# Hybrid encoder step on one core: all attention projections beside stick-breaking, the recurrence started in the forgetting attention, and smaller staging edits

## The chip, the cores and the metric

The kernel runs on one NeuronCore of a Trainium2 chip. The metric is the device time of one execution in microseconds (us), the median over several runs. Engines are named as the profile names them: PE is TensorE's matmuls and PEld its weight loads, DVE is VectorE, ACT is ScalarE, POOL is GpSimd, and SP is the sync engine, which here only issues DMAs.

## The reference

One layer of a streaming encoder is computed for 1024 prompt rows and 64 sample rows of width 1024; the two groups share all weights, and the sample group has 256 cached rows. Cut to what matters:

```
u = rms_norm(x)
proj = u @ w_in            # q, k, v of three attentions, the inputs of the delta net, four gates of width 1024
A forgetting attention (fox): softmax(q k' / 8 + c_q - c_k), causal, c = cumsum(log_sigmoid(f))
B differential attention (diff): softmax1 - lam * softmax2, block-causal in chunks of 64, then rms_norm
C stick-breaking attention (sb): exp(log_sigmoid(z) + reversed cumsum of log_sigmoid(-z)), strictly causal
D gated delta net (gdn): conv, silu, l2norm, then per chunk of 64 rows:
    solve (I + m) sol = [v beta, k beta exp(g)]          # a triangular solve
    v_new = u_i - kc_i S;  o = q_i S + a_i v_new;  S = S exp(g_last) + k_i' v_new      # a recurrence over chunks
merged = sum_b sigmoid(gate_b) * (o_b @ w_branch[b])
x += merged @ w_out;  x += (silu(h wg) * (h wu)) wd, h = rms_norm(x);  y = rms_norm(x)
```

The new k, v, log-forget rows, the last state S and the last conv rows are outputs as well.

## The kernel before

All 1088 rows of u lie in SBUF as two f16 halves (a high part and a rest), and weights are split in the same way when they are loaded: `load_unit` reads a block of 256 columns, ACT writes `wh`, and DVE writes the rest `wl`. So each product is made of three matmuls.

The program has these stages. First come the norm, the projection of the delta net (`gdn_project`) and its first pass (`gdn_pass1`). Then come the three attentions in the order sb, fox, diff. Each attention loops over two pairs of heads, over nine row blocks in the order QORD (the long ones first), and over the two heads of the pair. For one head, PE makes the scores (`psc`), ACT and DVE make the weights (`st`), a transposing DMA issued by SP turns them (`pt`), and PE multiplies them with v (`pv` for sb and fox, `po` for diff). Behind the attentions comes the merge, in which each branch is multiplied by its branch weights (`ptb`), by its gate, and added into `mg`; then the output product (`pout`), the FFN and the last norm.

Three kinds of work have no fixed stage. `project(b)` makes q, k and v of an attention in 26 pieces of 24 matmuls of 256 columns; `put_q`, `put_k` and `put_v` split each piece with ACT and DVE, and SP writes it to DRAM. `spill_gates` makes the gates of all four branches in 96 pieces of 24 matmuls of 360 or 364 columns (`pgs`, lines 183 to 185); ACT copies each to a tile `ths`, and POOL writes it to DRAM, from where the merge reads it as `thg`. These two kinds are generators in the list `dense`. The list `side` has `gdn_solve`, the 30 steps of the triangular solve on DVE (tile X), and `gdn_seq`, the recurrence over 17 chunks, which makes small matmuls (`py`, `pu`, `pk`, `pog`, `pds`) and short DVE and ACT operations in turn. At each head (diff) or row block (sb, fox), `fill(us)` takes so many microseconds' worth of pieces from `dense`, by hand-set prices of 2.6 for a projection piece and 3.7 for a gate piece, and one step from `side`:

```
    def fill(us):
        debt[0] += us
        debt[0] = min(debt[0], us + 4.0)
        while dense and debt[0] > 0:
            c = next(dense[0], None)
...
        if side and next(side[0], None) is None:
            side.pop(0)
```

What is still in `dense` behind the attentions is issued by `drain(dense)`. The order that results from the code is only a priority: a scheduler places the instructions of each engine at build time, and on the chip each engine then works strictly in that order.

PSUM has eight banks: two for projections and gates (`pd`), three for scores (`psc`), one for `pv` and `po` (`pso`), and two for the delta net (`pgd`). SBUF pools are stacks: a pool opened in the place of a closed one has to wait for the last use of the old tiles.

Of the kernel before, what the change touches and what calls it, by code (L numbers as in the profile page):

```python
# [11 lines left out]
F32 = mybir.dt.float32  # L12
# [5 lines left out]
P = 128  # L18
D = 1024
KD = D // P  # L20
# [22 lines left out]

QORD = (7, 6, 5, 4, 3, 2, 8, 1, 0)

FILL_SB, FILL_FOX, FILL_DIFF, FILL_GDN = 0.0143, 0.0085, 0.0155, 8


def rows(t):
# [4 lines left out]
def tile_hybrid_encoder(ctx, tc, i, o):  # L54
# [809 lines left out]
    def gdn_solve():  # L864


        NP = 17 * NH
        with tc.tile_pool(name="gp2", bufs=1, side="right", reuse_waits="tile") as g2p:
            X = g2p.tile([NP, 2, 32, 32], F32, name="X")
            tmp = g2p.tile([NP, 512], F32, name="tmpx")  # L870
            gps.dma_start(X.rearrange("p b j i -> p b (j i)"), nd[0:17, :, 0:2].rearrange("n h b j i -> (n h) b (j i)"))
            for _ in range(3):
                yield 0.0
            for j in range(1, 31):
                r = 31 - j
                behind = tc.issue_after(at_mark[0].ins) if j == 1 else ExitStack()
                behind.__enter__()
                tj = tmp[:, :2 * j * r].rearrange("p (b c i) -> p b c i", b=2, c=j)
                tt(tj, bc(X[:, :, 0:j, j:j + 1], [NP, 2, j, r]), bc(X[:, :, j:j + 1, j + 1:32], [NP, 2, j, r]), ALU.mult)
                tt(X[:, :, 0:j, j + 1:32], X[:, :, 0:j, j + 1:32], tj, ALU.add)  # L880
                behind.__exit__(None, None, None)
                if j % 3 == 0:
                    yield 0.0
            for q in range(2):
                vec.memset(X[:, q].rearrange("p j i -> p (j i)")[:, 0:1024:33], 1.0)
            gps.dma_start(xd, X.rearrange("p b j i -> p (b j i)"))
            for q in range(2):
                vec.tensor_copy(tmp.rearrange("p (i j) -> p i j", j=32),
                                X[:, 0, :, 16 * q:16 * q + 16].rearrange("p j i -> p i j"))
                gps.dma_start(xtd[:, 512 * q:512 * q + 512], tmp)  # L890
# [2 lines left out]
        acopy(Sh, S32, 16.0)  # L893
        stt(Sl, S32, 16.0, Sh, ALU.mult, ALU.subtract)

    def gdn_seq(g3):
        ttbd = []
        for q in range(2):
            a = g3.tile([P, 2, NH, P], F16, name=f"ttbd{q}")
# [94 lines left out]
        for k, t in enumerate(order):  # L994
            after = load(order[k + 1]) if k + 1 < len(order) else None
            _, n, nch, u0, kc, kd, aa, qe, zt = here
            z4g = zt.rearrange("p (h e) -> p h e", h=NH)
            S32 = S32s if t == 8 else S32p
            if t in (8, 0):
                Sh, Sl = fresh_state()  # L1000
                new_state(S32, Sh, Sl)
            po = pgd("pog")
            pks = po[:, 256:512]
            for c in range(nch):
                sl = slice(64 * c, 64 * c + 64)
                e4 = eg[:, c, t * NH:(t + 1) * NH]
                for h in range(NH):
                    pe.matmul(pks[sl, h * 64:h * 64 + 64], lhsT=kc[:, h, sl], rhs=Sh[:, h], start=True, stop=False)
                    pe.matmul(pks[sl, h * 64:h * 64 + 64], lhsT=kc[:, h, sl], rhs=Sl[:, h], start=False, stop=True)
                S1 = g3.tile([P, NH, 64], F32, tag="S1", name="S1", bufs=2)  # L1010
                tt(S1, S32, bc(e4[:, :, None], [P, NH, 64]), ALU.mult)
                vn = g3.tile([P, NH, 64], F32, tag="vn", name="vn", bufs=2)
                vh = vhs[c]
                stt(vn[sl].rearrange("p h e -> p (h e)"), pks[sl, 0:256], -(2.0 ** -5),
                    u0[sl].rearrange("p h e -> p (h e)"), ALU.mult, ALU.add)
                acopy(vh[sl, 0], vn[sl])
                tt(vh[sl, 1], vn[sl], vh[sl, 0], ALU.subtract)
                pds = pgd("pds")
                for h in range(NH):
                    for q, (a, b) in enumerate(((0, 0), (0, 1), (1, 0))):  # L1020
                        pe.matmul(pds[:, h * 64:h * 64 + 64], lhsT=kd[:, a, h], rhs=vh[:, b, h], start=(q == 0), stop=(q == 2))
                for h in range(NH):
                    dst = po[sl, h * 64:h * 64 + 64]
                    pe.matmul(dst, lhsT=qe[:, h, sl], rhs=Sh[:, h], start=True, stop=False)
                    pe.matmul(dst, lhsT=qe[:, h, sl], rhs=Sl[:, h], start=False, stop=False)
                    pe.matmul(dst, lhsT=aa[:, 0, h], rhs=vh[:, 0, h], start=False, stop=False)
                    pe.matmul(dst, lhsT=aa[:, 0, h], rhs=vh[:, 1, h], start=False, stop=False)
                    pe.matmul(dst, lhsT=aa[:, 1, h], rhs=vh[:, 0, h], start=False, stop=True)
                stt(S32.rearrange("p h e -> p (h e)"), pds[:, 0:256], 2.0 ** -9, S1.rearrange("p h e -> p (h e)"), ALU.mult, ALU.add)
                Sh, Sl = fresh_state()  # L1030
                if not (t == 8 or (t == 7 and c == 1)):
                    new_state(S32, Sh, Sl)
                if c == 0 and after is not None:
                    here = prepare(*after)
                yield 0.0
            if t == 8:
                gps.dma_start(o["s_gdn_state"][0, 0].rearrange("h d e -> d h e"), S32[0:64])
            if t == 7:
                gps.dma_start(o["p_gdn_state"][0, 0].rearrange("h d e -> d h e"), S32[0:64])
            sq = g3.tile([P, NH, 64], F32, tag="sqo", name="sqo", bufs=1)  # L1040
            pov = po[:n, 0:256].rearrange("p (h e) -> p h e", h=NH)
            act.activation(sq[:n], pov, AF.Square)
            ss = g3.tile([P, NH], F32, tag="sso", name="sso", bufs=2)
            vec.tensor_reduce(out=ss[:n], in_=sq[:n], op=ALU.add, axis=AX.X)
            ts(ss[:n], ss[:n], 2.0 ** -18 / 64, EPS, ALU.mult, ALU.add, eng=gps)
            tt(ss[:n], ss[:n], mhb[:n, 0:NH], ALU.pow, eng=gps)
            tt(z4g[:n], z4g[:n], bc(ss[:n, :, None], [n, NH, 64]), ALU.mult)
            tt(z4g[:n], z4g[:n], pov, ALU.mult)
            os_ = g3.tile([P, 2, BW], F16, tag="osg", name="osg", bufs=2)
            acopy(os_[:n, 0], zt[:n])  # L1050
            tt(os_[:n, 1], zt[:n], os_[:n, 0], ALU.subtract)
            gps.dma_start(od["gdn"][t * P:t * P + n], os_[:n].rearrange("p l c -> p (l c)"))
# [3 lines left out]
    def spill_gates(b, sp, d2):  # L1056
        j = bidx[b]
        wu = load_unit([(w_in, 0, OFF_GATE + j * D + d2 * BW, BW)], BW)
        for m in range(2):
            d = 2 * d2 + m  # L1060
            for off, n in PIECES:
                pg = pd("pgs")
                gemm_a(pg, wu, m * P, uh, ul, off, n, KD)
                th = sp.tile([P, 364], F32, tag="ths", name="ths", bufs=2)
                with tc.high_priority():
                    acopy(th[:, :n], pg[:, :n], 0.5 * IWS)
                gps.dma_start(gtd[b][d * P:(d + 1) * P, off:off + n], th[:, :n])
                yield 3.7


    with tc.tile_pool(name="gp1", bufs=1, side="right", reuse_waits="tile") as g1p:
# [6 lines left out]
        gdn_project(xg)  # L1078
        ahead.clear()
        proj = [project(b) for b in ("sb", "fox", "diff")]  # L1080
        dense += proj[0:2]
        for w in gdn_pass1(g1p, xg):
            fill(w * FILL_GDN)
    drain(dense, proj[0])
# [6 lines left out]
    fill(16.0)  # L1091
    with tc.issue_after(pre.ins):
        attend_sb()
    drain(dense, proj[1])
    drain(dense, dense[0])
    cb_ = ExitStack()
    cb = cb_.enter_context(tc.tile_pool(name="cb", bufs=1, side="right", reuse_waits="tile"))
    dense.insert(0, proj[2])
    side.append(gdn_solve())
    attend_fox()  # L1100
    drain(dense, proj[2])
    drain(side)
    cb_.close()
    pj_.close()
    gd_, br_ = ExitStack(), ExitStack()
    g3 = gd_.enter_context(tc.tile_pool(name="gp3", bufs=1, side="right", reuse_waits="tile"))
    brps, branch = [], {}

    def load_branch(b):
# [8 lines left out]
        wbh = brp.tile([P, 2, D], F16, tag="wbh", name="wbh", bufs=2)  # L1118
        wbl = brp.tile([P, 2, D], F16, tag="wbl", name="wbl", bufs=2)
        for k in range(2):  # L1120
            w32 = wp.tile([P, 4, BW], F32, tag="w32", name="wb32", bufs=3)
            wv = w32.rearrange("p a b -> p (a b)")[:, :D]
            sync.dma_start(wv, i["w_branch"][0][j, k * P:(k + 1) * P])
            acopy(wbh[:, k], wv, WS)
            stt(wbl[:, k], wv, WS, wbh[:, k], ALU.mult, ALU.subtract)
# [2 lines left out]
    def open_merge():  # L1128
# [1 line left out]
        brps.append(br_.enter_context(tc.tile_pool(name="br", bufs=1, side="right", reuse_waits="tile")))  # L1130
        load_branch("sb")
        yield 0.0
        load_branch("fox")
        yield 0.0

    side += [gdn_seq(g3), open_merge()]
    attend_diff()
    drain(side)
    brp = brps[0]
# [17 lines left out]

    pbk = (psc, pgd, psc, pgd, psc)
    nb_ = [0]
    mg = [(brp if d < 3 else gt_pool).tile([P, T], F32, tag=f"mg{d}", name=f"mg{d}") for d in range(KD)]  # L1160
    order = ("sb", "fox", "diff", "gdn")
    for bi, b in enumerate(order):
        if b not in branch:
# [375 lines left out]
```

## Time and profile before

| | |
|---|---|
| time, median of 3 runs | 1920.94 us (1919.0 to 1921.34) |
| the profiled execution | 1923.47 us, of which the span from first to last instruction is 1921.5 us |
| mean granted TensorE clock | 0.954 of full speed |
| busy share of the span | PE 92%, PEld 65%, DVE 65%, ACT 45%, POOL 16% |

Busy shares are averages over stages with different limits, and a matmul's recorded time overlaps that of the next one. So the stages have to be read one by one: which engine is busy in each, at what clock, and what the others wait for.

### The profile page before, as it was taken

What the parts mean: (1) busy time and instruction counts of PE and PEld (TensorE: products, weight loads), DVE (VectorE), ACT (ScalarE), POOL (GpSimd) and SP (SyncE); (2) the same over time, 40 slices, a digit from 0 to 9 for tenths busy, and PEclk for the clock granted to TensorE, in tenths of its full rate; (3) what the DMA queues carried; (4) which work ended last, traced back from release to release, by engine and by line L of the source; (5) the groups of instructions that cost most, each with busy time, mean ns of one, the idle gap of its engine ahead of it and who ended that gap; (6) DMA issues with size and microseconds to landing.
All of it is one profiled execution on the core that took longest, in us unless ns stands there. A gap on an engine that the chain in (4) does not pass through costs nothing.

```text
span 1921.5 us, 36810 instructions
## 1 busy us (share of the span) xinstructions
PE 1767.0 (92%) x14364; PEld 1252.4 (65%) x14364; DVE 1249.0 (65%) x2589; ACT 868.2 (45%) x1819; POOL 310.3 (16%) x478
## 2 busy tenths in 40 slices
PE   7999898989977998766799889999999999999998
PEld 5678774656755565444466558886857758677573
DVE  7559773877776667889411997766646546556365
ACT  6335654998654455556522463433413314233142
POOL 2113341111001222212211661000000000000002
PEclk9999999999989999566899999999999999999999
DMA  6267789887989855444733955621211212112112
GB/s 222 44 108 218 224 234 215 168 179 155 208 191 210 183 148 128 94 108 84 262 107 103 280 153 144 121 83 34 78 44 45 67 32 79 45 45 67 33 45 99
DMA packets 412766, 244.28 MB, mean 127 GB/s; under 512 B 266278, under 2 KB 390450, under 8 KB 412456
## 3 DMA queue, kind: packets, MB, share of 16 engines
q1 hardware_dynamic: 398944, 205.67, 43.9%
q0 software_dynamic: 13648, 36.27, 6.5%
q8 instruction: 112, 1.84, 0.4%
q14 instruction: 62, 0.51, 0.1%
HBM read 123.39 MB, written 60.53 MB: 96 GB/s over the span
## 4 chain that ended last, share of the span: by engine, by line
PE 53%; DVE 8%; DMA 7%; issue 2%; ACT 1%; POOL 1%; SPq 0%; DVEq 0%; POOLq 0%; ACTq 0%
PE po L1461 12%; DMA pt<-st 4%; PE pgs L185 4%; PE pgs L183 3%; PE pgs L184 3%; PE pb L1345 3%; PE pb L1344 3%; PE pb L1346 3%; PE pc L1345 2%; PE pc L1346 2%; PE pa L1346 2%; PE pc L1344 2%; PE pa L1345 2%; PE pa L1344 2%; PE pout L165 1%
## 5 line engine op out<-in xcount | busy, mean ns | idle before, releaser
L183 PE MATMUL pgs<-u,wh 128*128 128x364 f16 (+1 forms) x768 | 245.1, 319 | 10.0 <-ACT ths L61 9.7
L184 PE MATMUL pgs<-u,wh 128*128 128x364 f16 (+1 forms) x768 | 245.2, 319 | 0.0
L185 PE MATMUL pgs<-u,wl 128*128 128x364 f16 (+1 forms) x768 | 244.7, 319 | 0.5 <-DVE wl L64 0.5
L1461 PE MATMUL po<-wh,hT 128*128 128x512 f16 (+1 forms) x792 | 238.1, 380 | 0.6 <-DVE x2a L64 0.6
L1461 PEld LDWEIGHTS <-hT 128*128 128x128 f16 (+1 forms) x1188 | 109.2, 99 | 120.0 <-issue 7.6
L64 DVE SCALAR_TENSOR_TENSOR x2a<-po,x2a 128x512 f32<-128x512 f32 x108 | 74.4, 689 | 141.6 <-PE po L1461 141.4
L61 ACT ACTIVATE wh<-w32f 128x1024 f16<-128x1024 f32 (+1 forms) x90 | 80.3, 926 | 160.6 <-PE po L1461 111.6
L1344 PE MATMUL pb<-X,wh 128*128 128x288 f16 (+1 forms) x528 | 147.1, 279 | 2.5 <-DMA X<-nsh 2.2
L1345 PE MATMUL pb<-X,wh 128*128 128x288 f16 (+1 forms) x528 | 147.2, 279 | 0.3 <-DMA X<-nsl 0.3
L1346 PE MATMUL pb<-X,wl 128*128 128x256 f16 (+1 forms) x528 | 146.3, 279 | 0.0
L64 DVE SCALAR_TENSOR_TENSOR wl<-w32f,wh 128x1024 f16<-128x1024 f32 (+1 forms) x90 | 94.6, 1065 | 79.2 <-ACT wh L61 79.1
L64 DVE SCALAR_TENSOR_TENSOR wl<-w,wh 128x1024 f16<-128x1024 f32 x62 | 74.8, 1229 | 108.8 <-ACT wh L61 80.3
L1461 PE MATMUL po<-wl,hT 128*128 128x512 f16 (+1 forms) x396 | 142.0, 379 | 0.0
L1344 PEld LDWEIGHTS <-wh 128*128 128x128 f16 x1232 | 120.5, 98 | 31.1 <-issue 2.3
L1345 PEld LDWEIGHTS <-wh 128*128 128x128 f16 x1232 | 120.5, 98 | 30.0 <-issue 2.4
L1346 PEld LDWEIGHTS <-wl 128*128 128x128 f16 x1232 | 120.5, 98 | 27.2 <-issue 0.9
L184 PEld LDWEIGHTS <-wh 128*128 128x128 f16 x912 | 89.6, 98 | 61.0 <-issue 11.8
L165 PE MATMUL pd<-wh,u 128*128 128x256 f16 (+1 forms) x448 | 123.8, 276 | 1.5 <-ACT e L61 1.5
L167 PE MATMUL pd<-wh,u 128*128 128x256 f16 (+1 forms) x448 | 123.5, 276 | 0.0
L166 PE MATMUL pd<-wl,u 128*128 128x256 f16 (+1 forms) x448 | 123.5, 276 | 0.0
L183 PEld LDWEIGHTS <-wh 128*128 128x128 f16 x912 | 89.7, 98 | 51.7 <-issue 1.7
L185 PEld LDWEIGHTS <-wl 128*128 128x128 f16 x912 | 89.6, 98 | 51.4 <-issue 1.2
(393 smaller groups left out, 4647.4 us busy)
## 6 DMA issues: line engine op xcount, KB each, us to landing
w<-in_w_in_dram SPq DMA_DIRECT2D x56, 512.0 KB, 5.3
w32f<-in_w_ffn_gate_dram SPq DMA_DIRECT2D x20, 512.0 KB, 4.9
w32f<-in_w_ffn_up_dram SPq DMA_DIRECT2D x20, 512.0 KB, 3.9
w32f<-in_w_ffn_down_dram SPq DMA_DIRECT2D x20, 512.0 KB, 4.1
xt<-in_x_prompt_dram SPq DMA_DIRECT2D x8, 512.0 KB, 6.8
wb<-in_w_branch_dram SPq DMA_DIRECT2D x8, 512.0 KB, 4.9
w<-in_w_out_dram SPq DMA_DIRECT2D x8, 512.0 KB, 4.9
x2a<-in_x_prompt_dram SPq DMA_DIRECT2D x8, 512.0 KB, 8.4
```

Source lines behind the costliest of these rows:

```text
L61: return act.activation(out, in_, AF.Copy, scale=scale)
L64: return vec.scalar_tensor_tensor(out=out, in0=in0, scalar=s, in1=in1, op0=op0, op1=op1)
L165: pe.matmul(ps[:n, :N], lhsT=a, rhs=wh[:, k, :N], start=(k == 0), stop=False)
L166: pe.matmul(ps[:n, :N], lhsT=a, rhs=wl[:, k, :N], start=False, stop=False)
L167: pe.matmul(ps[:n, :N], lhsT=b, rhs=wh[:, k, :N], start=False, stop=(k == K - 1))
L183: pe.matmul(ps[:, :n], lhsT=a, rhs=xh[:, k, off:off + n], start=(k == 0), stop=False)
L184: pe.matmul(ps[:, :n], lhsT=a, rhs=xl[:, k, off:off + n], start=False, stop=False)
L185: mm = pe.matmul(ps[:, :n], lhsT=b, rhs=xh[:, k, off:off + n], start=False, stop=(k == K - 1))
L1344: pe.matmul(ps[:, :n], lhsT=wh[:, k], rhs=xh_, start=(start and k == 0), stop=False, skip_group_check=not start)
L1345: pe.matmul(ps[:, :n], lhsT=wh[:, k], rhs=xl_, start=False, stop=False, skip_group_check=not start)
L1346: mm = pe.matmul(ps[:, :n], lhsT=wl[:, k], rhs=xh_, start=False, stop=(k == 3), skip_group_check=not start)
L1461: pe.matmul(ps[h * n:h * n + n], lhsT=hts[k + h][:, a, tk:tk + n], rhs=w[:, k + h], start=(k == 0 and a == 0 and w is wh), stop=(k + nh >= ...
```

## The change

- `dense` gets all three projections at the start; before, that of diff was put in front of the list when the fox attention began. All of them now end within the sb attention, and their pool `pj` is closed there.
- `gdn_solve`, `gdn_seq` and `open_merge` stand in `side` from the start of the fox attention on; before, `gdn_seq` was put there when the diff attention began. The solve has fewer yields (2 for 3, and one in 4 steps for one in 3). The fill of the fox attention falls from 0.0085 to 0.006 per column.
- `pds`, the product for the state's update, no longer takes a bank of its own, but lies in the second half of that of `pog`.
- `ths` has four buffers for two. The branch weights of sb are staged in the tiles of `mg0` and `mg1`, `mg2` moves to another pool, and the branch weights of fox are no longer loaded ahead of the merge's loop.

```diff
-FILL_SB, FILL_FOX, FILL_DIFF, FILL_GDN = 0.0143, 0.0085, 0.0155, 8
+FILL_SB, FILL_FOX, FILL_DIFF, FILL_GDN = 0.0143, 0.006, 0.0155, 8
...
-            for _ in range(3):
+            for _ in range(2):
                 yield 0.0
             for j in range(1, 31):
...
-                if j % 3 == 0:
+                if j % 4 == 0:
                     yield 0.0
...
-    def gdn_seq(g3):
+    def gdn_seq(stack):
+        g3 = stack.enter_context(tc.tile_pool(name="gp3", bufs=1, side="right", reuse_waits="tile"))
...
             po = pgd("pog")
-            pks = po[:, 256:512]
+            pks = pds = po[:, 256:512]
...
-                pds = pgd("pds")
...
-                th = sp.tile([P, 364], F32, tag="ths", name="ths", bufs=2)
+                th = sp.tile([P, 364], F32, tag="ths", name="ths", bufs=4)
...
         proj = [project(b) for b in ("sb", "fox", "diff")]
-        dense += proj[0:2]
+        dense += proj
...
         attend_sb()
-    drain(dense, proj[1])
     drain(dense, dense[0])
-    cb_ = ExitStack()
-    cb = cb_.enter_context(tc.tile_pool(name="cb", bufs=1, side="right", reuse_waits="tile"))
-    dense.insert(0, proj[2])
-    side.append(gdn_solve())
-    attend_fox()
-    drain(dense, proj[2])
-    drain(side)
-    cb_.close()
     pj_.close()
     gd_, br_ = ExitStack(), ExitStack()
-    g3 = gd_.enter_context(tc.tile_pool(name="gp3", bufs=1, side="right", reuse_waits="tile"))
+    cb = gd_.enter_context(tc.tile_pool(name="cb", bufs=1, side="right", reuse_waits="tile"))
...
-            w32 = wp.tile([P, 4, BW], F32, tag="w32", name="wb32", bufs=3)
-            wv = w32.rearrange("p a b -> p (a b)")[:, :D]
+            if b == "sb":
+                wv = brp.tile([P, T], F32, tag=f"mg{k}", name="wb32")[:, :D]
+            else:
+                w32 = wp.tile([P, 4, BW], F32, tag="w32", name="wb32", bufs=3)
+                wv = w32.rearrange("p a b -> p (a b)")[:, :D]
...
         load_branch("sb")
         yield 0.0
-        load_branch("fox")
-        yield 0.0
-
-    side += [gdn_seq(g3), open_merge()]
+
+    side += [gdn_solve(), gdn_seq(gd_), open_merge()]
+    attend_fox()
     attend_diff()
...
-    mg = [(brp if d < 3 else gt_pool).tile([P, T], F32, tag=f"mg{d}", name=f"mg{d}") for d in range(KD)]
+    mg = [(brp if d < 2 else gt_pool).tile([P, T], F32, tag=f"mg{d}", name=f"mg{d}") for d in range(KD)]
```

How the order on the engines moves is seen at three places. The first is ACT in the first half of the sb attention; `z`, `e`, `st` and `os` are the attention's own rows, and the numbers behind `e` tell projection tiles apart. Before:

```order
L61 ACTIVATE ths<-pgs 128x364
L536 ACTIVATE e<-z 128x640
L61 ACTIVATE st<-z 128x768
L537 ACTIVATE e<-e 128x640
L544 ACTIVATE z<-z 128x768
L61 ACTIVATE z<-psc 128x512
L538 ACTIVATE e<-e 128x640
L61 ACTIVATE os<-pv 128x128
```

With the change, at the same row block:

```order
L61 ACTIVATE e_4642<-pd 128x256
L536 ACTIVATE e<-z 128x640
L61 ACTIVATE ks<-e_4642 128x8x64
L537 ACTIVATE e<-e 128x640
L61 ACTIVATE e_4675<-pd 128x256
L61 ACTIVATE z<-psc 128x512
L61 ACTIVATE z<-psc 128x128
L544 ACTIVATE z<-z 128x768
L538 ACTIVATE e<-e 128x640
L61 ACTIVATE ks<-e_4675 128x8x64
```

One copy of a gate piece is replaced by two operations for each projection piece. The second place is ACT in the second pair of heads of the diff attention, where `p`, `st`, `t`, `sq` and `osd` are the attention's rows, and `vh`, `Sh` and `ttbd` those of the recurrence. Before:

```order
L61 ACTIVATE osd<-o_12125 128x128
L61 ACTIVATE vh_8741<-vn 64x256
L655 ACTIVATE p,sm_12456<-psc,sm_12456 128x512
L655 ACTIVATE p,sm_12456<-psc,sm_12456 128x256
L61 ACTIVATE t_12453<-po 128x64
L61 ACTIVATE Sh<-S32p 128x256
L61 ACTIVATE st<-p,sm_12456 128x768
L61 ACTIVATE vh_8743<-vn 64x256
```

With the change, at the same row block:

```order
L61 ACTIVATE ths<-pgs 128x364
L614 ACTIVATE sq<-o_11889 128x128
L655 ACTIVATE p,sm_12248<-psc,sm_12248 128x512
L655 ACTIVATE p,sm_12248<-psc,sm_12248 128x256
L61 ACTIVATE wh<-w_13437 128x1024
L61 ACTIVATE wh<-w_13441 128x1024
L61 ACTIVATE osd<-o_11889 128x128
L61 ACTIVATE ths<-pgs 128x360
L61 ACTIVATE vh_7843<-vn 64x256
L61 ACTIVATE ttbd_7831<-tt_7835 64x4x64
```

Gate pieces and the split of their weights now stand between the rows of attention and recurrence, where there were none. The third place is PE behind the last row of the diff attention. Before, the branch products `ptb` of sb begin, and these rows are where they break off for the drained gates:

```order
L185 LDWEIGHTS wbl
L185 MATMUL ptb<-oT,wbl 128x360
L183 LDWEIGHTS wh
L183 MATMUL pgs<-u_103,wh 128x364
L184 LDWEIGHTS wh
L184 MATMUL pgs<-u_103,wh 128x364
```

With the change, the first branch product follows the last gate matmul of the program:

```order
L185 LDWEIGHTS wl
L185 MATMUL pgs<-u_103,wl 128x360
L183 LDWEIGHTS wbh
L183 MATMUL ptb<-oT,wbh 128x364
L184 LDWEIGHTS wbh
L184 MATMUL ptb<-oT,wbh 128x364
```

Counted in the two programs' PE order, the 2304 gate matmuls are spread like this (the stages are told apart by the mask matmul of each attention):

| gate matmuls | up to sb's start | sb | fox | diff | behind diff |
|---|---|---|---|---|---|
| before | 143 | 721 | 106 | 614 | 720 |
| with the change | 0 | 432 | 415 | 1457 | 0 |

Of the 648 projection matmuls of diff, 600 full ones and 48 of half the array, all stand in the fox attention before; with the change, 144 stand ahead of sb, and 504 in its first half.

## Rows read from the trace of the kernel before

**Rows 1.** The span in 40 equal slices: busy tenths of PE, its granted clock.
```profile
PE   7999898989977998766799889999999999999998
PEclk9999999999989999566899999999999999999999
```

**Rows 2.** Windows by stage: length, each engine's busy us (instructions), clock, DMA share, GB/s.
```profile
core 0: us, PE busy (x) PEld busy (x) DVE busy (x) ACT busy (x) POOL busy (x), PEclk, DMA share, GB/s
310.00:480.00 170.00, 161.78 (x1405) 102.69 (x1405) 129.63 (x191) 152.42 (x300) 31.15 (x50) 1.00 0.83 175
480.00:630.00 150.00, 124.80 (x1271) 94.01 (x1270) 109.14 (x338) 80.10 (x175) 15.52 (x24) 0.93 0.94 202
630.00:760.00 130.00, 128.23 (x1196) 82.52 (x1194) 87.57 (x254) 65.56 (x168) 32.85 (x55) 1.00 0.65 150
760.00:915.00 155.00, 102.40 (x1107) 74.62 (x1107) 136.83 (x500) 87.08 (x268) 36.45 (x60) 0.60 0.46 101
915.00:1055.00 140.00, 129.08 (x824) 81.03 (x822) 31.32 (x45) 46.70 (x85) 23.72 (x42) 0.95 0.47 160
1055.00:1145.00 90.00, 78.00 (x491) 47.59 (x490) 80.12 (x123) 48.24 (x92) 56.55 (x51) 0.98 0.76 222
987.00:1034.00 47.00, 47.00 (x308) 29.92 (x307) 6.00 (x7) 10.55 (x19) 6.50 (x12) 1.00 0.31 105
```

**Rows 3.** The same windows for the gates' tile pgs alone: PE, ACT, clock, DMA.
```profile
310.00:480.00 170.00, 122.97 (x744) 15.63 (x33) 1.00 0.83 175
630.00:760.00 130.00, 101.44 (x605) 12.22 (x26) 1.00 0.65 150
760.00:915.00 155.00, 0.00 (x0) 0.00 (x0) 0.60 0.46 101
915.00:1055.00 140.00, 111.30 (x718) 13.51 (x29) 0.95 0.47 160
```

**Rows 4.** Who PE waited for, 630 to 760 us: total, times, longest.
```profile
PE po L604 <- DMA pt<-st: 0.6, 1, 0.6
```

**Rows 5.** Groups by line, whole span: count, busy us, mean ns, idle before.
```profile
L61 ACT ACTIVATE ths<-pgs 128x364 f32<-128x364 f32 (+1 forms) x96 | 45.0, 469 | 82.6 <-PE pgs L185 38.0 <-DMA gtd_sb<-ths 22.9 <-issue 17.5
L61 ACT ACTIVATE e<-pd 128x256 f32<-128x256 f32 (+1 forms) x41 | 15.4, 376 | 16.1 <-PE pd L167 14.9 <-DVE qs L64 0.9
L61 ACT ACTIVATE ks<-e 128x256 f16<-128x256 f32 (+3 forms) x27 | 13.0, 484 | 0.5
L61 ACT ACTIVATE vs<-e 128x256 f16<-128x256 f32 (+1 forms) x27 | 10.8, 411 | 4.0 <-DMA vd_sb<-vs 2.7 <-DMA vd_fox<-vs 0.9
L61 ACT ACTIVATE qs<-pd 128x512 f16<-128x512 f32 (+1 forms) x17 | 10.1, 593 | 14.8 <-PE pd L167 12.5 <-DMA qd_sb<-qs 2.3
L64 DVE SCALAR_TENSOR_TENSOR wl<-w,wh 128x1024 f16<-128x1024 f32 x62 | 74.8, 1229 | 108.8 <-ACT wh L61 80.3 <-PE pgs L185 28.2
```

**Rows 6.** DMA issues by line: count, KB each, us to landing.
```profile
w<-in_w_in_dram SPq DMA_DIRECT2D x56, 512.0 KB, 5.3
...
gtd_fox<-ths POOLq DMA_DIRECT2D x16, 182.0 KB, 3.4
...
kd_diff<-ks SPq DMA_DIRECT2D x10, 256.0 KB, 3.7
...
qd_diff<-qs SPq DMA_DIRECT2D x8, 256.0 KB, 2.7
...
vd_diff<-vs SPq DMA_DIRECT2D x10, 128.0 KB, 3.3
...
out_p_diff_k_dram<-e SPq DMA_DIRECT2D x8, 128.0 KB, 2.7
```

**Rows 7.** Groups by line, PE alone, 480 to 630 us.
```profile
L468 PE MATMUL pv<-pt,vt 128*64 128x128 f16 (+2 forms) x420 | 18.8, 231 | 19.1 <-DMA pt<-st 17.3 <-DVE mn L71 1.8
```

**Rows 8.** Who PE waited for, 760 to 915 us: total, times, longest.
```profile
PE po L604 <- DMA pt<-st: 15.7, 11, 3.6
PE psc L456 <- ACT p L655: 10.9, 18, 1.8
```

## The prediction

> **What bounds the kernel now.** I read the slices of the span first. PE is busy nearly everywhere, but four slices, from about 770 to 960 us, have only 5, 6, 6 and 8 tenths of the clock [rows 1]. So I cut the span at the mask products of the attentions and read the stages one by one [rows 2].
>
> In the sb attention (310 to 480) ACT is busy 152 of 170 us and PE 162. Both are nearly full; ACT is the one without slack in its rows. In the fox attention (480 to 630) no engine is full (PE 125, DVE 109 of 150 us), but the DMA share is 0.94, and PE waits 17.3 us for transposed weights [rows 2, 7]. Here the diff projections and the transposes share the DMA engines. The diff attention has two parts. From 630 to 760 PE is full at the full clock and waits 0.6 us in all [rows 2, 4]. From 760 to 915 PE has no gate matmul left [rows 3], runs at a mean clock of 0.60, and DVE is busy 137 of 155 us; PE waits for transposes and for ACT in turn [rows 8]. Then, from 915 to 1055, 718 gate matmuls run almost alone: PE full, DVE 31 and ACT 47 of 140 us [rows 2, 3].
>
> So PE's filler is in the wrong place: 155 us with too little for PE are followed by 140 us with nothing else. Across the five windows the question is how much of the drained 720 gate matmuls fits under the attentions, and what the projections, now in sb, cost there.
>
> **Prices.** A full-clock stretch of 308 matmuls of 360 or 364 columns takes 47.0 us: 0.153 us each [rows 2]. A projection matmul has 256 columns; by columns I put it at 0.107 us, an estimate. The window 630 to 760 has 605 gate matmuls (92.6 us) and 591 others, which fill the remaining 37.4 us, so 0.063 each, small recurrence matmuls, scores and products together [rows 2, 3]. A gate piece of 24 matmuls costs ACT 0.469 us; a k piece costs 0.376 + 0.484, a v piece 0.376 + 0.411, a q piece 0.593 [rows 5]. A block of weights (144 gate matmuls) costs DVE 2 x 1.229 us [rows 5].
>
> **Sb: +18 us.** Out go 721 - 432 = 289 gate matmuls (44 us of PE), in come 504 of the projections (54 us): PE +10. On ACT, 9 k pieces, 9 v pieces, 3 q evictions and 4 cache blocks come in: 18 x 0.376 + 11 x 0.484 + 11 x 0.411 + 3 x 0.593 = 18.4 us; 12 gate copies go out, 5.6 us. ACT goes from 152 to 165 us, and at the old share of 152/170 that is a stage of 184: +14. On DMA, k and v rows and the two outputs, about 6.0 MB, and 0.5 MB of q come in, 2.2 MB of gates go out [rows 6]; at 211 GB/s (175 at share 0.83) that is +20 on 141 us, a share of 0.86. That lies nearer the old 0.83 than fox's 0.94, so I add only 4 us for it. Bounds: 0, if all of it hides, and +32, if the 17.3 us of DMA waits of fox come along. The 144 matmuls ahead of sb take the place of 143 gate matmuls, and I put them at nothing: sb's first scores wait there for k and v from DRAM anyway (the DMA engines carry the load of the first pass until 310).
>
> **Fox: -30 us.** PE has 415 gate matmuls (63 us) and 517 others (33 us): 96 us. DMA work was 0.94 x 150 = 141 us. Out go 8.1 MB of projection rows and 3.1 MB of projection weights, in come 2.4 MB of gates and 2.3 MB of gate weights (309 more gate matmuls) [rows 6]; net 6.6 MB at 215 GB/s, 31 us, leaves 110. DMA is still the longest, at its old share 117; I take 120, since both ends of a stage carry less. Bounds: 100 (PE alone) and 150 (no gain). The solve on DVE only changes its pace.
>
> **Diff: +40 us.** PE has 1457 gate matmuls (223 us) and about 1614 others (102 us): 325, against 285 now. DVE has 88 + 137 = 224 us, and 852 more gate matmuls bring 5.9 blocks of weights, 14.5 us: 239, or 74% of 325. So PE is the bound, as it was from 630 to 760 with nearly the same mixture. Bounds: 310, if the fox products that now stand in this stage cover part of it, and 415, if all 852 x 0.153 = 130 us come in series.
>
> **Behind diff: -114 us.** The drain (140) and the rest of the merge (90) hold 576 branch products (88 us of PE). DVE's part is 80 us there and 31 in the drain, of which 12 are gate weights: 99 us, and at the old 80/90 that is 111. In the drain, sb's products and the weights' staging were hidden under the gates; that cover is gone, and this is why not all of the 140 us come back. 5 us are for the start, in which the merge's pool waits for the attention's tiles. So 116 for 230. Bounds: 105 and 130.
>
> **Edits at nothing.** The four `ths` buffers, the staging of sb's weights in `mg` tiles and fox's branch weights lie under gates or other branches; without that cover one branch's weights are two loads of 5 us. The shared bank of `pds` shortens waits for a bank or lengthens the chain of the recurrence; either hides under PE-bound gates. The recurrence hardly moves into fox at all: in DVE's order its first `vn` stands behind the second head's `st` of diff, and behind the first one before. So this part of the change does not do what its words say, and I give it 0. It ends earlier, though, behind head 29 of 36 instead of at the end.
>
> **The sum.** +18 - 30 + 40 - 114 = -86. The span of 1921.5 us becomes 1835.5; with the 2 us around it the execution takes 1837.5, and as the profiled one is 2.5 us above the median of the runs, I forecast **1835 us**.
>
> On the bank there is a rule that speaks against the change. The recurrence's state update on DVE reads `pds`, and PE writes `pog` in the same bank for 20 more matmuls of each chunk; at 0.063 us that would be 17 x 20 x 0.063 = 21 us on the chain. The Trainium skill (PSUM — Partial Sum Buffer, "PSUM bank collisions raise a hardware error") says that two engines must be kept apart on one bank and quadrant even where their columns differ, so DVE has to wait for those matmuls. By the rule, and if that chain were the bound, the sum would be 1856; by the window of 630 to 760, in which PE never waits for the recurrence, it is 1835.
>
> **The rivals.**
> - *The projections choke sb* (0.15). ACT, PE and DMA all near full there, so sb takes the +32, and fox, whose transposes queue behind late writes, only falls to 135: 1835 + 14 + 15 = 1864, and up to 1900 with diff worse by some 30. For it: ACT's 152 of 170. Against: fox now runs with these pieces at 0.94, and waits only 17 us.
> - *The clock falls in fox* (0.07). Before, PE was busy 125 of 150 us there at 0.93, and 102 of 155 at 0.60 in the thin part of diff. PE's 96 of 120 lie nearer the first. At 0.60 its 96 us would be 160: 1835 + 40 = 1875. The Trainium skill (TensorE: Matmul & The Clock Gate, "Part 1: The HAM clock gate") says that the slow clock is the default and activity releases it; no run here shows which of the two levels so broken a stream gets.
> - *The recurrence in lockstep behind the gates* (0.06), the slower case. Each of 17 chunks crosses PE some four times, and each crossing can stand behind a gate piece of 24 x 0.153 = 3.7 us: 250 us, if nothing covers them. With 160 of them uncovered diff takes 445 and the kernel 1955. It is slower than before from a diff stage of 414 us on, that is with half of these waits bare. Against it stand the 0.6 us of waits in the window that had gates and recurrence together [rows 4].
> - *Better than the sum* (0.14). Sb hides the projections (-18), fox falls to 105 (-15), the merge takes 108 (-8): 1794.
>
> **How the numbers follow.** The forecast, 1800 to 1862 around 1835, has 0.56; the better case 0.14; the two middle rivals 0.22, at 1862 to 1917; within 0.2% of before, which is about what a measurement of this kernel can tell from no change, 0.02; slower 0.06. Faster is 0.56 + 0.14 + 0.22 = 0.92. The range leaves out most of the better case's lower half and the upper part of the middle rivals: 1795 to 1885.
>
> **What would show it.** Right: gate matmuls in every window of diff, at a clock near 1.0, with PE's waits small; diff near 325 us; no stretch of gates alone behind it; branch products in about 115 us with DVE near 0.9; fox shorter at a DMA share still over 0.9; ACT over 0.85 in sb. Wrong: a diff stage over 380 us with PE waiting for DVE or ACT, a clock under 0.8 in fox, or an sb stage over 205 us. The sum fails first if DVE's 239 us and PE's 325 us in diff do not overlap as they did from 630 to 760.

## The result, and the profile after

The changed kernel takes **1811.53 us** (median of three runs; 1808.83 to 1816.62), where the kernel before took 1921.14 on the same chip: a ratio of 0.9429, 95% interval 0.9393 to 0.9465. A fourth run took 5692 us, for no reason that the record shows, and is left out; counted in, it makes the median 1814.07. The profiled execution took 1816.62 us with a span of 1814.9, at a mean clock of 0.988. The forecast of 1835 (1795 to 1885) was 23 us too slow (21 by the other median).

The slices of the changed kernel's span, PE's busy tenths and its granted clock; in [rows 1] four slices fell to 5, 6, 6 and 8 tenths of the clock:

```profile
PE   7999898888998899999988899999999999999998
PEclk9999999998999999999999999999999999999999
```

The thin part is gone. The stages lie elsewhere now, so the windows are cut at the new mask products: sb, fox, diff, behind diff. First all work (columns as in [rows 2]; the DMA share is the view's figure and can read slightly over 1), then the gates' tile `pgs` alone (PE, ACT, clock, DMA):

```profile
302.00:492.00 190.00, 166.57 (x1531) 116.78 (x1529) 136.38 (x210) 158.43 (x318) 22.07 (x36) 0.95 0.85 182
492.00:600.00 108.00, 100.43 (x930) 62.50 (x929) 88.34 (x285) 63.06 (x135) 19.96 (x33) 0.98 1.02 204
600.00:926.00 326.00, 318.69 (x3207) 213.72 (x3206) 255.13 (x791) 189.51 (x496) 95.88 (x159) 1.00 0.69 164
926.00:1038.00 112.00, 94.79 (x590) 57.27 (x590) 88.50 (x155) 65.72 (x134) 59.01 (x58) 0.98 0.84 255
```

```profile
302.00:492.00 190.00, 73.98 (x432) 7.95 (x17) 0.95 0.85 182
492.00:600.00 108.00, 71.36 (x415) 7.74 (x17) 0.98 1.02 204
600.00:926.00 326.00, 243.84 (x1457) 28.46 (x61) 1.00 0.69 164
926.00:1038.00 112.00, 0.00 (x0) 0.45 (x1) 0.98 0.84 255
```

Diff is 326 us with 1457 gate matmuls at the full clock and PE busy for 319; there are no gates behind it. DVE is busy 88.5 of the last 112 us. Who PE waited for, in sb, in diff and behind diff:

```profile
PE pv L468 <- DMA pt<-st: 20.3, 8, 8.3
```

```profile
PE po L604 <- DMA pt<-st: 2.7, 2, 1.5
PE psc L456 <- ACT p L655: 1.4, 1, 1.4
```

```profile
PE ptb L183 <- DVE thg L64: 11.8, 15, 1.9
PE ptb L183 <- DVE mg L64: 3.4, 5, 1.9
```

In diff the 15.7 and 10.9 us of [rows 8] are down to 2.7 and 1.4. In sb, transposed weights are now waited for 20.3 us; in the kernel before it was 6.6 us (314.9 to 472.4).

**What held the gates up before.** The prediction read where the gate matmuls stood, not why they stopped at 760 us. The loads tell it. In the kernel before, by the tiles `w` (weights of gates, 640 to 760 us, then 918 to 1000) and `wb` (branch weights, the same two windows); durations in ns, then the first and last start:

```profile
L149 SPq DMA_DIRECT2D w<-in_w_in_dram x3: 390/522/1262, 643.6 to 670.2; - x3
...
L149 SPq DMA_DIRECT2D w<-in_w_in_dram x10: 383/383/457, 925.5 to 986.9; - x10
```

```profile
L1123 SPq DMA_DIRECT2D wb<-in_w_branch_dram x3: 333/357/400, 672.1 to 698.8; - x3
...
L61 ACT ACTIVATE wbh<-wb x4: 1038/1038/1057, 919.5 to 933.4; 128x1024 f16<-128x1024 f32 x4
```

No gate weight is loaded between 670.2 and 925.5 us. `load_branch` stages its blocks in the ring `w32`, three slots that gate weights use too. Two blocks of sb and one of fox take all three. They are released when ACT writes `wbh`, into a pool that can open only when the recurrence's pool `gp3` is closed. The recurrence's last state update started at 913.9 (the last `S32p`):

```profile
L64 DVE SCALAR_TENSOR_TENSOR S32p<-pds,S x16: 403/416/425, 703.2 to 913.9; 128x256 f32<-128x256 f32 x16
```

The first `wbh` follows 5.6 us later. In the changed kernel sb's blocks lie in the `mg` tiles, fox's aren't loaded ahead, and gate weights are loaded all through diff (`w`, 640 to 760 and 760 to 918):

```profile
L149 SPq DMA_DIRECT2D w<-in_w_in_dram x8: 394/424/752, 643.4 to 744.3; - x8
...
L149 SPq DMA_DIRECT2D w<-in_w_in_dram x5: 392/400/1263, 777.2 to 838.9; - x5
```

### The profile page after: what moved, and what is told of

It reads as the page before. It is cut to its first block, busy times and chain, and to the rows that moved or that the text cites. A ratio compares the mean times of both kernels' runs of the same rounds, so it can differ in the third digit from the quotient of the medians.

```text
span 1814.9 us, 36826 instructions
## 1 busy us (share of the span) xinstructions
PE 1723.7 (95%) x14364; PEld 1224.8 (67%) x14364; DVE 1246.7 (69%) x2589; ACT 866.9 (48%) x1819; POOL 307.0 (17%) x478
## 4 chain that ended last, share of the span: by engine, by line
PE 55%; DMA 6%; DVE 5%; issue 2%; ACT 1%; POOL 1%; SPq 0%; DVEq 0%; POOLq 0%; ACTq 0%
PE po L1454 12%; PE pgs L183 4%; PE pgs L185 4%; PE pgs L184 4%; PE pb L1337 3%; PE pb L1339 3%; PE pb L1338 3%; DMA pt<-st 3%; PE pa L1339 2%; PE pc L1338 2%; PE pa L1338 2%; PE pa L1337 2%; PE pc L1339 2%; PE pc L1337 2%; DMA thg<-gtd_sb 1%
```

## The experiments

The theory formed from these rows: the staging holds the gates up, the recurrence's end holds the merge up, and moving the projections is worth little. The rival: the projections' move is the gain. The table holds all kernels; the stage times (us) are read from each profile at the first mask product of sb, fox and diff, the last `po` and the first `pout`. "Behind" begins at the last `po` here, so it is shorter than the windows from the last gate. Each ratio is to runs of the kernel before on the same chip at the same time, whose median was 1921 to 1927 us.

| kernel | median us | ratio to before (95%) | sb starts | sb | fox | diff | behind |
|---|---|---|---|---|---|---|---|
| before | 1921.14 | 1 | 314.9 | 157.5 | 153.9 | 288.6 | 229.3 |
| changed | 1811.53 | 0.9429 (0.9393 to 0.9465) | 302.1 | 189.4 | 108.7 | 336.6 | 100.9 |
| 1 before, no fox preload | 1850.94 | 0.9655 (0.9606 to 0.9704) | 313.9 | 158.3 | 151.1 | 313.2 | 137.3 |
| 2 changed, staging undone | 1912.34 | 0.9965 (0.9931 to 0.9999) | 304.6 | 184.9 | 106.4 | 368.8 | 170.5 |
| 3 before, projections early | 1918.14 | 1.0013 (0.998 to 1.0046) | 315.6 | 169.4 | 138.1 | 287.2 | 225.7 |
| 4 changed, loads spaced | 1818.06 | 0.9474 (0.9435 to 0.9513) | 303.5 | 181.0 | 110.8 | 343.9 | 103.8 |
| 5 changed, recurrence late | 1820.54 | 0.9464 (0.9421 to 0.9508) | 300.2 | 185.7 | 114.6 | 336.2 | 107.7 |
| 6 changed, own bank | 1846.38 | 0.9599 (0.9566 to 0.9633) | 302.0 | 183.7 | 110.6 | 335.4 | 137.3 |
| 7 as 1, projections early | 1867.35 | 0.9717 (0.9663 to 0.977) | 327.6 | 166.3 | 136.6 | 324.8 | 133.2 |
| 8 changed, two `ths` | 1809.71 | 0.9405 (0.9368 to 0.9441) | 301.4 | 183.8 | 105.7 | 338.6 | 102.6 |
| 9 as 1, shared bank | 1838.62 | 0.9578 (0.9536 to 0.9621) | 320.7 | 158.0 | 147.0 | 331.1 | 99.7 |
| 10 as 9, loads spaced | 1837.42 | 0.9564 (0.9537 to 0.9592) | 301.2 | 160.9 | 151.2 | 344.9 | 99.8 |
| 11 before, shared bank | 1902.8 | 0.9906 (0.9875 to 0.9937) | 307.6 | 160.3 | 151.7 | 352.3 | 145.9 |
| 12 changed, old fill | 1845.3 | 0.9571 (0.9539 to 0.9603) | 309.1 | 183.3 | 155.8 | 319.2 | 101.2 |

The stage times are of one profile each. The kernel before, 1, 9 and 11 differ only behind sb, and sb starts between 307.6 and 320.7 in them; the changed one, 5, 6 and 12 also differ only behind sb, and there it starts between 300.2 and 309.1 and takes 183.3 to 189.4, most in the changed one, whose profiled execution was the longest of its three. Differences of a few us in one stage are not read by themselves.

**1. One line of the kernel before.**

```diff
         load_branch("sb")
         yield 0.0
-        load_branch("fox")
-        yield 0.0
```

> The kernel before with one thing changed: the branch weights of fox are no longer loaded ahead of the merge. Theory S (the staging ring was full: two branches staged four blocks in a ring of three slots, and gate weights could not pass): the 720 gate matmuls behind diff move under it, as the program's order now has them (1334 in diff, none behind). Diff 1334 x 0.153 + 1666 x 0.063 = 309 us for 288, the merge about 115 for 229, the rest as before: about 1825 us. Theory P (moving the projections made the room, and the staging is worth nothing): within 10 us of before, 1911 to 1925.

It took 1850.94: nearer the staging theory than the rival, but 26 us short of its forecast. Two `wb` loads stand at 669 to 694 us instead of three, one slot of the ring is left to the gates, and that is enough: `w` loads go on (7 up to 760, 6 more up to 918). Gate matmuls, from 626 us on:

```profile
626.00:760.00 134.00, 105.67 (x628) 12.16 (x26) 0.99 0.65 158
760.00:937.00 177.00, 120.30 (x702) 14.06 (x30) 0.97 0.60 143
937.00:1074.00 137.00, 0.00 (x0) 0.00 (x0) 0.89 0.74 229
```

This one line is three fifths of the whole gain (ratio lower by 0.0345, of 0.0571). What is missing lies behind diff. The recurrence has slipped to the very end, and the first branch product waits for the pool (its operand `oT` lies in it):

```profile
L64 DVE SCALAR_TENSOR_TENSOR S32p<-pds,S x16: 415/424/425, 700.0 to 946.0; 128x256 f32<-128x256 f32 x16
```

```profile
PE ptb L183 <- DMA oT<-od_sb: 12.0, 1, 12.0
```

From 937 to 959 us PE is busy 6.4 of 22 us.

**2. The staging undone in the changed kernel.** Sb's blocks go through the ring again, and fox's are loaded ahead.

```diff
-            if b == "sb":
-                wv = brp.tile([P, T], F32, tag=f"mg{k}", name="wb32")[:, :D]
-            else:
-                w32 = ...
+            w32 = ...
...
         load_branch("sb")
         yield 0.0
+        load_branch("fox")
+        yield 0.0
```

> The changed kernel with the staging of branch weights as before (sb through the ring of three, fox loaded ahead of the merge). Theory S: the order has 449 gate matmuls in diff and 1008 behind it; 1008 x 0.153 = 154 us come back as a stretch of gates alone, diff is at most 50 us shorter, so about 1905 to 1930 us. Theory P: within 10 us of the changed kernel, 1804 to 1824.

1912.34: nearly the whole gain is gone, though the projections, the bank, the fill and the recurrence stay as changed. Windows of this kernel:

```profile
700.00:800.00 100.00, 63.51 (x740) 46.93 (x740) 87.35 (x309) 54.06 (x161) 23.89 (x39) 0.65 0.49 111
800.00:865.00 65.00, 38.75 (x423) 28.20 (x422) 56.83 (x197) 38.88 (x110) 14.68 (x24) 0.63 0.45 95
865.00:965.00 100.00, 96.46 (x625) 60.55 (x626) 31.08 (x86) 34.90 (x81) 20.01 (x34) 0.96 0.53 158
```

The thin part, with its clock of 0.65 and 0.63, is back, and ends as `wbh` is first written, at 860.9.

**3. The projections alone, in the kernel before.**

```diff
-        dense += proj[0:2]
+        dense += proj
...
-    dense.insert(0, proj[2])
```

> The kernel before with all three projections at the start of the list and nothing else. Theory S: 720 gate matmuls stay behind diff; sb about 20 us longer, fox about 35 to 45 shorter, the rest as before: 1895 to 1910 us. Theory P: most of the 107 us appears here, under 1860 us.

Nothing: 1.0013. Fox falls by 16 us and sb grows by 12. Sb and fox were expected to move more, and the time misses the ranges of both theories; the rival falls, as the gain does not come from this edit by itself.

**4. The crowd of loads in sb.** In the changed kernel the two `ckb` broadcasts and the load of X are issued within 1.1 us at 405 us, since their pool opens when the projections' pool closes. They, and what is issued beside them (v of fox among it, 640 KB), land late (issues from 404 to 408 us: KB each, us to landing):

```profile
ckb<-ckd POOLq DMA_DIRECT2D x2, 672.0 KB, 11.4
...
X<-nd POOLq DMA_DIRECT2D x1, 544.0 KB, 15.2
...
pt<-st SPq DMA_TRANSPOSE x1, 18.6
```

The median `pt` lands in 4.3 us. The edit spreads the three over 456 to 484 us.

```diff
+                behind = od_at["sb", 1, (3, 8)[hp]] if pair == 0 else None
+                with tc.issue_after(behind.ins) ...:
                     gps.dma_start(ckb[:, hp], ...)
```

> The changed kernel with the two broadcast loads of the forget sums (ckb) and the load of the solve put behind later rows of the second pair of sb on the POOL queue. Theory B (the burst of these three loads at 405 us is what made sb 32 us longer: transposes took 17 to 19 us to land, PE idled 12 us there): sb 12 to 20 us shorter, 1795 to 1805 us. Rival (sb is longer because ACT has the projections' copies): sb stays within 5 us, 1809 to 1818 us.

The window 395 to 440 us of the changed kernel, and then of this one:

```profile
395.00:440.00 45.00, 33.19 (x230) 19.77 (x228) 27.70 (x28) 30.85 (x49) 7.57 (x13) 0.85 0.99 201
```

```profile
395.00:440.00 45.00, 39.73 (x321) 24.70 (x320) 35.52 (x37) 38.62 (x61) 7.80 (x13) 0.96 0.80 188
```

In this stretch 91 more matmuls run, and sb is 8 us shorter. But the profile of the changed kernel shows the burst at its worst: in 5, 6 and 12, which have the same burst, X lands after 10.4 to 11.0 us instead of 15.2, the same stretch holds 275 to 302 matmuls, and sb takes 183 to 186 us. Against these the spacing is worth 2 to 5 us of sb, so theory B, which asked for 12 to 20, falls. The total does not fall, much as the rival had it, though that ACT is the cause is not shown by this run. PE still waits 13.2 us for `pt` in sb (15.4 to 16.5 in 5, 6 and 12), and diff is 7 us longer.

**5. The recurrence put in the list behind fox, as before.**

```diff
-    side += [gdn_solve(), gdn_seq(gd_), open_merge()]
+    side += [gdn_solve()]
     attend_fox()
+    side += [gdn_seq(gd_), open_merge()]
```

> The changed kernel, with the recurrence and the opening of the merge put in the list only behind the fox attention, as before. By the order the recurrence still ends behind head 29 of 36, and 120 gate pieces' matmuls move behind diff (18 us), which shorten diff by as much. Theory O, the starting place does nothing by itself: 1812 to 1822 us, last recurrence operation within 10 us of the changed kernel's distance to the end of diff. Rival R, the early start is what lets the merge begin on time: the branch products start 15 us or more later behind the last po, 1830 to 1850.

1820.54, within what theory O allowed; its interval overlaps that of the change. Its last state update starts at 895.7, and at 903.3 in the changed kernel. So the starting place by itself does nothing that can be measured. In the changed kernel the recurrence does not run in fox at all, in spite of its place in the list: its first `vn` starts at 643.3 us, 43 us into diff, and before the change it was 35 us into diff (661.2).

**6. A bank of its own for `pds`.**

```diff
-            pks = pds = po[:, 256:512]
+            pks = po[:, 256:512]
...
+                pds = pgd("pds")
```

> The changed kernel, with pds in a PSUM tile of its own again. By the order the recurrence then ends behind head 36 instead of 29 of the diff attention, and no gate moves. Theory K, the shared bank is what lets the merge start on time: the first branch product waits for the recurrence's end and for the tiles of its pool, 15 to 30 us as in the run without fox's preload, 1828 to 1845. Rival N, the bank is hidden under PE-bound gates, as the prediction put it: 1808 to 1820. The rule on two engines at one bank would make this kernel faster than the changed one: below 1805.

1846.38, just over theory K's range and far from both others: the shared bank is worth about 33 us (0.0170 of 1921). The recurrence's last update and the first use of branch weights, in the changed kernel and then in this one:

```profile
L64 DVE SCALAR_TENSOR_TENSOR S32p<-pog,S x16: 349/423/426, 671.0 to 903.3; 128x256 f32<-128x256 f32 x16
```

```profile
L64 DVE SCALAR_TENSOR_TENSOR S32p<-pds,S x16: 407/422/425, 680.0 to 943.1; 128x256 f32<-128x256 f32 x16
```

```profile
PE ptb L183 <- ACT wbh L61: 14.8, 1, 14.8
```

```profile
926.00:959.00 33.00, 9.32 (x131) 7.69 (x130) 13.07 (x35) 14.50 (x34) 10.39 (x17) 0.59 0.61 211
```

With its own bank the recurrence ends 40 us later, behind the attention instead of in it. For 33 us PE is busy 9.3, at a clock of 0.59, until the merge's pool is free.

**7. All projections early, with the preload gone (on top of 1).** Both diffs, 1 and 3.

> The kernel before, without fox's preload of branch weights and with all projections put in the list at the start. Gates 432 in sb, 547 in fox, 1325 in diff, none behind. The run without the preload alone took 1850.9. Theory S, the projections' move only shifts work between sb and fox, and the late recurrence costs the rest: 1843 to 1858. Rival P, the move pays once gates can flow (fox shorter by 25 us or more, sb not longer by as much): 1815 to 1835.

1867.35, outside both ranges and above kernel 1 (the intervals just overlap). Sb starts 14 us later here, where X lands after 30 us instead of 17, and diff is 12 us longer; the last update of the recurrence starts at 957.6. With fox at the old fill and the bank apart, the early projections bring nothing, or a loss.

**8. Two `ths` buffers.** `bufs=4` becomes 2 in the changed kernel.

> The changed kernel with two buffers of ths instead of four. A gate piece takes PE 3.7 us, its copy on ACT 0.47, and its way to DRAM about 3.4 us, so two buffers give each some 7 us: theory N, nothing, 1809 to 1820. Rival T, where the transfers are crowded (sb's burst, landing times of 10 us and more) the copies wait, and with them PE and ACT: sb longer by 5 us or more, 1822 to 1835.

1809.71; the intervals overlap. The four buffers are worth nothing.

**9. Two edits on the kernel before: 1, and the shared bank.**

> The kernel before with two of the change's edits: no preload of fox's branch weights, and pds in the bank of pog. Gates 721 in sb, 106 in fox, 1334 in diff, none behind; by the order the recurrence ends behind head 25 instead of 36. Theory K, these two are the whole gain: the 1850.9 of the run without the preload less the 33 us by which the late recurrence held up the merge, 1810 to 1828. Rival P, what is still missing there comes from the projections' move: 1835 to 1851.

1838.62, in rival P's range: theory K's claim, that the two are the whole gain, falls. The merge does start on time (the last `S32p` at 910.0, "behind" 99.7). What is missing lies ahead of diff: diff begins at 625.7 us here and at 600.2 in the changed kernel. Of these 25 us, 19 are the later start of sb in this profile, and 7 lie in sb and fox together: sb is 31 us shorter here and fox 38 longer. In fox the DMA engines are as good as full (478.7 to 625.7), where the changed kernel has 108 us at the same bound:

```profile
478.70:625.70 147.00, 126.11 (x1327) 96.26 (x1326) 112.03 (x346) 85.71 (x183) 15.49 (x24) 0.97 0.98 211
```

**10. The same with the three loads spaced as in 4.**

> The two edits, and the three loads for the solve and the forget rows (issued together at about 290 us before) put behind rows of sb's second pair on POOL. Theory B, sb's k and v no longer share the DMA engines with them, sb starts near 302 instead of 314 us, and nothing takes that back: 10 us below the run with the two edits, 1798 to 1815. Rival G, given back later, as where the same loads were spaced in the changed kernel: within 4 us of the run with the two edits.

Sb starts at 301.2 instead of 320.7 (313.9 in kernel 1) and diff at 613.3 instead of 625.7, and the kernel is no faster: 0.9564 against 0.9578. PE waits for `pt` in diff for 11.2 us (3.0 in kernel 9), the recurrence ends at 918.3, and diff is 14 us longer. Rival G holds.

**11. The shared bank alone.**

> The kernel before with pds in the bank of pog and nothing else; fox's preload still holds the gates up, 720 of them behind diff by the order, while the recurrence ends behind head 25. Theory K, without gates to fill with, the earlier end brings little: diff falls by less than 10 us, 1908 to 1922. Rival V, the bank's 33 us come in any kernel: 1880 to 1893. By the rule on two engines at one bank it is slower: above 1930.

1902.8, below theory K's range, yet far from 33 us. The gates wait as in the kernel before, but for a shorter time, since the ring's slots come free with the recurrence. Loads of `w` and the first `wbh` (both 760 to 918 us):

```profile
L149 SPq DMA_DIRECT2D w<-in_w_in_dram x7: 367/379/598, 885.9 to 907.9; - x7
```

```profile
L61 ACT ACTIVATE wbh<-wb x4: 1043/1046/1057, 880.9 to 894.7; 128x1024 f16<-128x1024 f32 x4
```

The recurrence's last update is at 870.2, 43.7 us ahead of the kernel before; `wbh` follows 38.6 us earlier, the gate weights 39.6 us earlier. This run shows the chain from recurrence to `wbh` to gate weights by moving its first link.

**12. The old fill of the fox attention.** `FILL_FOX` is 0.0085 again in the changed kernel.

> The changed kernel with the fill of the fox attention at 0.0085 again. By the order 607 gates stand in fox instead of 415, 1169 in diff instead of 1457, 96 behind diff. Theory E, with PE the bound in all three places the work only changes its place: fox 192 x 0.153 = 29 us longer, diff 44 shorter, behind diff up to 15 longer, 1808 to 1822. Rival F, the lower fill is what keeps fox short, and the stage loses more than PE's time, as it did with 547 gates and the projections moved alone (138 us): fox over 140 us and diff not shorter by as much, 1830 to 1850.

1845.3, as rival F said. Gate matmuls that run in fox are missing at the end of diff. Windows of this kernel, 139 us that hold most of fox, and the end of diff:

```profile
489.00:628.00 139.00, 127.32 (x1151) 79.97 (x1151) 104.15 (x316) 74.63 (x160) 28.30 (x47) 0.98 0.95 195
925.00:968.00 43.00, 30.90 (x202) 18.23 (x201) 34.56 (x137) 25.85 (x82) 10.08 (x18) 0.80 0.62 152
```

From 925 to 968 only 52 gate matmuls are left, and PE is busy 31 of 43 us at 0.80. From sb's first mask product to the first `pout` this kernel takes 759.5 us, the changed one 735.6: PE is idle 13 us longer and busy 11 us longer (690.7 and 680.1 us), while its matmuls are the same, 6246. Kernel 9 with the lower fill, but without the projections' move, was not run, so this does not show that the two need each other.

## Why the prediction came out as it did

The mechanism was right (gates under diff, PE the bound there, the merge alone behind it). The total came so near in part by luck, as the misses below offset each other: sb and diff came out 22 us over the forecast, fox, the merge and the part ahead of sb 42 us under it.

- **Diff: near.** 325 us forecast, 326 measured from 600 to 926, where the gates end, with PE 319 and 2.7 us of waits for transposes; up to the last `po`, where the stage ended in the forecast's own windows of before, it is 337, +48 for a forecast +40. DVE was 255 us, where 239 were forecast, and still not the bound.
- **Behind diff: near.** 116 forecast, 112 measured from the last gate, with DVE 88.5 us, a share of 0.79, where near 0.9 was to be the sign; from the last `po` it is 101, since the first branch products now run beside the end of diff.
- **Fox: too cautious by 15.** 120 us were forecast, from 110 us of DMA work at its old share. The work was 110 (108 x 1.02), the share rose from 0.94 to 1.02, and the stage took 108 (-45.2 by the table's marks).
- **Sb: the term that was mis-sized.** +18 forecast; by the table +31.9, which is the upper bound of +32, for the reason that it gave: PE waits 20.3 us for transposed weights. In the profiles of 5, 6 and 12 it is +26 to +28, with waits of 15.4 to 16.5 us. ACT came to 158 us and the DMA share to 0.85, close to the forecast 165 and 0.86. So no engine choked; PE, ACT and DMA were at 0.88, 0.83 and 0.85 of 190 us. By run 4 the burst is 8 us of it at most; the other waits stay unexplained.
- **Ahead of sb: taken as nothing, -12.8.** The burst stood there before, at 290 us, beside the load of sb's k and v, and moved into sb with the change. Loads issued from 288 to 292 us in the kernel before:

```profile
ckb<-ckd POOLq DMA_DIRECT2D x2, 672.0 KB, 16.7
...
kT<-kd_sb SPq DMA_TRANSPOSE x1, 17.6
```

Run 10, which spreads the same loads in a kernel that else starts like the old one, has sb start at 301 as well, where the four kernels with the burst at 290 start it at 308 to 321. That points to the burst, by one profile.

The steps add up to -12.8 + 31.9 - 45.2 + 48.0 - 128.4 = -106.5 by the table's marks, against -86.

**The step that failed is "Edits at nothing".** It took the new places of the gates as given and priced each staging edit by the work that it removes. But the places are what those edits buy. The sum was not harmed, since the gates were counted in the built order; the account of which edit does the work was. Undone in the changed kernel (difference of ratios, times 1921), the staging costs 103 us, the shared bank 33, the lower fill 27, the recurrence's start 7 and the `ths` buffers -5; the last two are within the intervals. The first three add up to 163 us for a gain of 110, so what one of them is worth depends on the others. Added alone to the kernel before, the preload's removal gives 66, the bank 18, the projections nothing. That `ths` and the recurrence's start are worth nothing was right.

**On the bank** the prediction weighed a rule (the Trainium skill, PSUM — Partial Sum Buffer, "PSUM bank collisions raise a hardware error"), by which DVE has to wait for the matmuls of `pog` in the same bank, and put it at 21 us. That wait is there, and small: in the last chunk the last matmul of `pog` starts 0.8 us behind the last of the state's product (902.3 and 901.5 us), where the rule's price was 1.3 a chunk. DVE's idle time for it in the changed kernel, 620 to 900 us:

```profile
DVE S32p L64 <- PE pog L1028: 4.0, 6, 1.6
```

With a bank of its own the same operation waits 5.6 us for `pds` (run 6, the same stretch). Sharing made the recurrence end 40, 36 and 44 us earlier in three pairs (changed and 6, 9 and 1, 11 and before). So neither "nothing" nor the rule's +21 held: it was worth 33 us when the gates flowed. It asks for one PSUM tile less in each chunk, out of two buffers; that this is what moved the recurrence forward in the built order is argued, not shown, since no single wait of that size shows in the rows.

**The projections' move** was priced as a shift between sb and fox, which runs 3 and 7 bear out. With the old fill the changed kernel (12, 0.9571) is level with the two edits alone (9, 0.9578), so without the lower fill the move buys nothing. A reading that fits, but is not shown, is that the move frees fox of DMA work, and the lower fill lets fox end early and keeps the gates for diff; whether the lower fill would do as much without the move was not run.

Of the rivals, "better than the sum" (1794) was nearest in fox and the merge, and "the projections choke sb" in sb; they offset each other in part. The clock stayed at 0.98 in fox, and the recurrence did not hold up the gates in diff (its rival's 445 us for diff adds 160 to the old stage of 285; on the forecast 325 it would be 485).

## What to carry to other kernels

When filler work stops early, look at the loads of its weights before its place in the program: a staging ring of three slots, three of them held by an early load whose consumer needs a pool that isn't open yet, looks like a scheduling problem and cost 66 to 103 us. When a change moves work, price each edit by taking it away from the new kernel as well as by adding it to the old one; here the staging was worth 103 us taken away and its main line 66 added, the bank 33 and 18, and the projections' move, added, nothing. And spread filler so that it lasts to the end of the last stage that has gaps: gates put into an earlier stage than needed cost 27 us, in idle time and in clock.

## What was not expected of the hardware

- Beside three loads of 544 to 672 KB issued within about 1 us, and one of 640 KB, a transpose landed after 18.6 us, where the median is 4.3, and a 64 KB write after 14.9 us. Spaced out (run 4), the three landed in 5.2 to 6.1 us.
- The granted clock fell where PE thinned out: 0.85 in the 45 us of the burst, 0.80 at the end of diff in run 12, 0.59 in the 33 us ahead of the merge in run 6. In the unbroken diff of the changed kernel it was 1.00.
- A gain ahead of diff was taken back in full in run 10: diff began 12 us earlier than in run 9, and nothing of it was left at the end. Why diff grew by what was saved ahead of it is only partly seen, in PE's waits for `pt` (11.2 us for 3.0), and stays open.
